# Token-major pieces of a gate stage: fixed order on vector and scalar engine, inverse roots as a one-column GpSimd power, early squares on the scalar engine

## The chip, the cores and the metric

The kernel runs on one core of one Trainium2 chip. A core has a matrix engine (TensorE, PE in the profile, with its weight loads as PEld), a vector engine (VectorE, DVE), a scalar engine for activation functions (ScalarE, ACT), a general engine (GpSimd, POOL), and SyncE (SP), whose queue issues nearly all transfers here. Each engine works through its own instructions in order and waits on semaphores for the others. The metric is the device time in microseconds (us), the median of several runs.

## The reference

One layer of a decoder block on x of 1024 tokens by 1024 features: a pooling mixer and a gated linear recurrence, an MLP with squared ReLU, a gated per-layer embedding, and a last RMS norm. What the change touches is the end:

```
z = rms_norm(h, norm_ple_g[l])
gate = jax.nn.sigmoid(z @ w_ple_gate[l] + b_ple_gate[l])
h = h + gate * (p[l] @ w_ple_proj[l])
...
return rms_norm(h, norm_final_g)
```

with `rms_norm(h, g) = h * rsqrt(mean(h * h) + 1e-6) * g`, the mean over the 1024 features of a token. All values are float32.

## The kernel before

Nearly everything is feature-major: `H[o]` holds feature block o (128 features on the partitions) for all 1024 tokens. Matrix products in float32 are made of three passes over operands split in a high and a low part (`split`, `mm`), which is why PE has the most work by far. A planner orders the instructions of each engine by their place in the program and by when their inputs are expected; what is wrapped in `keep_in_program_order` keeps the written order on its engine. The helper `pin` does that only while the list `in_order` is not empty.

The gate stage at the end runs in three parts.

1. First half of the tokens (group 0), feature-major, eight blocks: `ple_proj`, `ple_gate`, `ple_out`. The squares for the last norm are collected on the way.
2. Second half of the tokens (group 1), feature-major, but only the first four feature blocks, in the order 2, 3, 0, 1. In between, the first token half is scaled by its final norm (`finish`, called with the blocks that `DONE` lists) and stored (`store`, after blocks 3 and 7). The blocks of `H` for the second token half are turned token-major by `turn_block` (32 by 32 transposes), written to DRAM by `turn_out` and read back by `turn_in` as `late[i]`: 128 tokens on the partitions, 1024 features along the row. `quarter(i, 0)` is the row's early half (features that part 2 has finished), `quarter(i, 1)` its late half.
3. Second half of the tokens, late four feature blocks, token-major: four pieces i of 128 tokens. PE computes `token_proj` and `token_gate` of a piece into two PSUM banks. Then, per piece:
   - logits: gate product plus bias row (DVE, L1148), sigmoid (ACT, L1149), product with the projection (DVE, L1150), sum into the late half (`late_half`, DVE, L1143);
   - `early_half` for the early halves: a multiply-and-sum instruction on DVE gives the mean square plus epsilon (`mean`, L1109), then the early half is multiplied by its gains (L1117). It is called for pieces 0 and 1 in piece 0, for 2 in piece 1 and for 3 in piece 2;
   - `token_finish`: the mean square of the late half on top of the early one (`mean`), `root_of` (square root on ACT, L1155, then reciprocal on DVE, L1156), the early half scaled on ACT (L1163), the late half scaled by root and gains on DVE (L1164), and the store of the piece (L1165).

The last piece is `token_last`. Its gate product comes first, then its projection in two halves of 256 columns in banks of their own; the vector work follows in the same two halves, in written order, and the two halves of its output leave by separate stores (L1197). A one-column square root on `root` (L1175) makes ACT load the table of that function ahead of `root_of`.

PSUM banks are handed out in turn: pieces 0 and 2 use single banks, piece 1 a double one, and piece 3 three single banks. The means, roots and reciprocals are single columns of `spread`.

Of the kernel before, what the change touches and what calls it, by code (L numbers as in the profile page):

```python
# [31 lines left out]

ORDER = ((0, 1, 2, 3, 4, 5, 6, 7), (2, 3, 0, 1))

DONE = ((), (0, 1, 2), (3, 4), (5,), (6, 7), (), (), ())
FETCH = ((0, 1, 2, 3), (0, 1))
NTOK = 4
NQUAD = 4 * P
# [21 lines left out]
def block_kernel(  # L60
# [111 lines left out]
    def pin(ins):  # L172
        return tc.keep_in_program_order(ins) if in_order else ins
# [843 lines left out]
    rfin = T[5]  # L1017
    gate_p, held = {}, []
    ms = spread[:, 40 : 40 + 4 * NTOK]
    root = pool.tile([P, 1], F32, name="root")  # L1020

    def ple_psum(g, hs, o, apart):
        turn.append(o)
# [74 lines left out]
    def quarter(i, half):  # L1098
        return late[i][:, half * NQUAD : (half + 1) * NQUAD]
# [4 lines left out]
            quarter(i, half), bounce[half][i // 2][b : b + 4].rearrange("b t g x -> (b t) (g x)")  # L1104
        )

    def mean(i, x, before, to):

        nc.vector.tensor_tensor_reduce(  # L1109
            square[:, : x.shape[-1]] if len(x.shape) == 2 else square[:, :256].rearrange("p (g x) -> p g x", g=4),  # L1110
            x, x, 1.0 / D, before, ALU.mult, ALU.add, ms[:, to : to + 1],
        )

    def early_half(i):
        x = quarter(i, 0)
        mean(i, x, EPS, 4 * i)
        nc.vector.tensor_tensor(x, x, g_row[:, :NQUAD], ALU.mult)  # L1117

    def token_slice(i):
        return slice(HALF + i * P, HALF + (i + 1) * P)  # L1120
# [18 lines left out]
    def late_half(i, e, cut):  # L1139

        y = quarter(i, 1).rearrange("p (g o x) -> p g o x", g=4, x=32)[:, :, cut.start // P : cut.stop // P]
        e = e[:, cut].rearrange("p (o g x) -> p g o x", g=4, x=32)
        nc.vector.tensor_tensor(y, y, e, ALU.add)  # L1143

    def token_out_all(i, pg, pj):
        t, e = T[3 + i % 2][:, FIRST], T[3 + i % 2][:, SECOND]
        whole = slice(0, NQUAD)
        nc.vector.tensor_tensor(by(t, pg), got(pg), by(b_row, pg), ALU.add)  # L1148
        nc.scalar.activation(t, t, AF.Sigmoid)  # L1149
        nc.vector.tensor_tensor(by(e, pj), by(t, pj), got(pj), ALU.mult)  # L1150
        late_half(i, e, whole)

    def root_of(i):
        r = ms[:, 4 * i + 3 : 4 * i + 4]
        pin(nc.scalar.activation(r, ms[:, 4 * i + 2 : 4 * i + 3], AF.Sqrt))  # L1155
        pin(nc.vector.reciprocal(r, r))  # L1156
        return r

    def token_finish(i):
        mean(i, quarter(i, 1), ms[:, 4 * i : 4 * i + 1], 4 * i + 2)  # L1160
        r = root_of(i)
        x, y = quarter(i, 0), quarter(i, 1)
        nc.scalar.activation(x, x, AF.Identity, scale=r)  # L1163
        nc.vector.scalar_tensor_tensor(y, y, r, g_row[:, NQUAD:], ALU.mult, ALU.mult)  # L1164
        nc.sync.dma_start(token_out[:, i], late[i])  # L1165

    def token_last(i, pg, pj):

        t, e = T[3 + i % 2][:, FIRST], T[3 + i % 2][:, SECOND]
        cuts = slice(0, 256), slice(256, NQUAD)  # L1170
        in_order[:] = [True]
        for a, cut in enumerate(cuts):
            pin(nc.vector.tensor_tensor(t[:, cut], got(pg)[:, a], b_row[:, cut], ALU.add))
            pin(nc.scalar.activation(t[:, cut], t[:, cut], AF.Sigmoid))
        pin(nc.scalar.activation(root, t[:, -1:], AF.Sqrt))  # L1175
        at = 4 * i
        y = quarter(i, 1)
        for a, cut in enumerate(cuts):
            x = pj[a]
            pin(nc.vector.tensor_tensor(by(e[:, cut], x), by(t[:, cut], x), got(x), ALU.mult))  # L1180
            yv = y.rearrange("p (g o x) -> p g o x", g=4, x=32)[:, :, 2 * a : 2 * a + 2]
            ev = e[:, cut].rearrange("p (o g x) -> p g o x", g=4, x=32)
            pin(nc.vector.tensor_tensor(yv, yv, ev, ALU.add))
            pin(
                nc.vector.tensor_tensor_reduce(
                    square[:, :256].rearrange("p (g x) -> p g x", g=4),
                    *[y.rearrange("p (g x) -> p g x", g=4)[:, :, 64 * a : 64 * a + 64]] * 2,
                    1.0 / D, ms[:, at + a : at + a + 1], ALU.mult, ALU.add, ms[:, at + a + 1 : at + a + 2],
                )
            )  # L1190
        r = root_of(i)
        both = late[i].rearrange("p (h x) -> p h x", h=2)
        for cut in cuts:
            x, v = both[:, 0, cut], both[:, 1, cut]
            pin(nc.scalar.activation(x, x, AF.Identity, scale=r))
            pin(nc.vector.scalar_tensor_tensor(v, v, r, g_row[:, NQUAD:][:, cut], ALU.mult, ALU.mult))
            nc.sync.dma_start(token_out[:, i].rearrange("p (h x) -> p h x", h=2)[:, :, cut], both[:, :, cut])  # L1197
        in_order.clear()

    for g, hs in enumerate(GROUPS):  # L1200
        if g == 1:
            leave("ple")
            late[:] = space("late", 8, F32)
        for n, o in enumerate(ORDER[g]):
            pg, pj = ple_psum(g, hs, o, False)
            if g == 0 and n < 2:
                ple_gate(g, hs, o, pg, n == 1)
                held.append((o, pg, pj))
                if n == 0:
                    first_sums()  # L1210
                    continue
                for o, pg, pj in held:
                    ple_proj(hs, o, pj)
                for o, pg, pj in held:
                    ple_out(hs, o, pg, pj)
            else:
                ple_proj(hs, o, pj)
                ple_gate(g, hs, o, pg)
            if g == 0 and 1 <= n < 5:
                raw = wp.tile([P, S], F32, tag="raw", name=f"wg0_{n + 3}_raw")  # L1220
                nc.sync.dma_start(raw, w_gate[n + 3])
                x = slice((n - 1) * P, n * P)
                split(raw.rearrange("p (k x) -> p k x", k=NT), *(w[:, :, x] for w in quad))
            if g > 0 or n > 1:
                ple_out(hs, o, pg, pj, g == 0)
            if g == 0 and n > 0:
                for o in range(NT) if n == 1 else ():
                    norm2.add(H[o], SECOND)
                if n == 2:
                    norm2.rstd(R, norm2.sums((SECOND,)))  # L1230
                for o in LATER[n - 1]:
                    ple_in_normed(o, SECOND)
            if g == 1:
                for j in range(2):
# [12 lines left out]
                finish(DONE[n])  # L1247
                if n == 1:
                    nc.sync.dma_start(row[:, : S + NQUAD], rows.broadcast_to([P, S + NQUAD]))
    for i in range(NTOK):  # L1250
        end = i == NTOK - 1
        pg, pj = ple_psum(2, slice(0, NQUAD), i, end)
        if end:
            token_gate(i, pg)
            pj = [x[:, :256] for x in (pj, bank("ps_j_end"))]
            for a, x in enumerate(pj):
                token_proj(i, x, slice(256 * a, 256 * a + 256))
            token_last(i, pg, pj)
            continue
        token_proj(i, pj, slice(0, NQUAD))  # L1260
        token_gate(i, pg)
        token_out_all(i, pg, pj)
        for x in ((0, 1), (2,), (3,))[i]:
            early_half(x)
        token_finish(i)
        finish(DONE[4 + i])
    leave("late")
    leave("sums")
    leave("proj")
# [78 lines left out]
```

## Time and profile before

| | |
|---|---|
| median of 3 runs | 926.03 us (925.99 to 926.21) |
| profiled execution | 925.73 us, span 923.9 us |
| granted TensorE clock, mean | 0.996 |
| instructions in the span | 10987 |
| PE busy | 911.2 us (99%) |
| DVE busy | 763.7 us (83%) |
| ACT busy | 449.0 us (49%) |
| POOL busy | 5.6 us (1%), 7 instructions |

The span runs from the first to the last instruction of the profiled execution. A busy share is the engine's busy time over the span. In the rows of a timeline stand the start, the duration, the engine, the line of the program, the operation, what it writes and reads, the shape and how many instructions are merged into the row; in brackets, how long the engine had been idle before it and which instruction ended that idle time. "SPq" is SyncE's queue; its rows are the issue of transfers, not the transfers. In the table of groups the columns are busy time, mean duration in ns, and idle time before with its releaser.

### The profile page before, as it was taken

The numbers are of one execution on the slowest core, as the hardware profiler recorded it, in microseconds if no ns is written. First come the engines' busy times: TensorE is split into PE (matmuls) and PEld (weight loads), VectorE is DVE, ScalarE is ACT, GpSimd is POOL, SyncE is SP. The second block draws the span as 40 slices with busy tenths as digits, with TensorE's granted clock in tenths as the row PEclk, the third lists the DMA queues.
The fourth block names the chain that finished last, engine by engine and source line by source line (L and its number), as shares of the span: only waits on it lengthen the run. The fifth ranks groups of instructions, "written<-read, shape, count | busy, mean of one in ns | idle before, by whom it ended". The sixth has DMA issues, their size and how long they took to land.

```text
span 923.9 us, 10987 instructions
## 1 busy us (share of the span) xinstructions
PE 911.2 (99%) x4229; PEld 792.4 (86%) x4229; DVE 763.7 (83%) x921; ACT 449.0 (49%) x514; POOL 5.6 (1%) x7
## 2 busy tenths in 40 slices
PE   9999999999999999999999999999999999999994
PEld 7888888888888888888888888888888888888884
DVE  7997984669998888888888989979776579789656
ACT  7568892447543343334334554443444346555314
POOL 0000000002000000000000000000000000000000
PEclk9999999999999999999999999999999999999998
DMA  7211143112154355345434989366532441031452
GB/s 266 94 52 31 38 167 107 69 45 78 65 196 153 126 176 198 127 148 173 181 125 148 353 310 338 115 202 205 197 102 92 128 147 45 20 118 46 126 180 94
DMA packets 50036, 128.94 MB, mean 140 GB/s; under 512 B 4544, under 2 KB 10176, under 8 KB 49984
## 3 DMA queue, kind: packets, MB, share of 16 engines
q1 hardware_dynamic: 49840, 128.21, 40.7%
q8 instruction: 33, 0.54, 0.3%
q14 instruction: 19, 0.16, 0.1%
q10 hardware_dynamic: 144, 0.04, 0.0%
HBM read 92.58 MB, written 35.65 MB: 139 GB/s over the span
## 4 chain that ended last, share of the span: by engine, by line
PE 98%; DVE 1%; issue 0%; ACT 0%; ACTq 0%
PE ps_P_u L352 31%; PE ps_P_d L352 31%; PE ps_i L352 10%; PE ps_o L352 9%; PE ps_e L352 8%; PE ps_l L352 3%; PE ps_e L1126 2%; PE ps_j L352 1%; PE ps_g L566 1%; PE ps_p L352 1%; PE ps_l L482 0%; PE ps_j L1135 0%; DVE t L1109 0%; PE n_ps L418 0%; PE n_ps L419 0%
## 5 line engine op out<-in xcount | busy, mean ns | idle before, releaser
L352 PE MATMUL ps_P_d<-a,wd_P_hi 128*128 128x512 f32 x880 | 261.7, 379 | 0.0
L352 PEld LDWEIGHTS ps_P_d<-a,wd_P_hi 128*128 128x128 f32 x880 | 166.3, 189 | 23.6
L352 PE MATMUL ps_P_d<-a,wd_P_lo 128*128 128x512 f32 x440 | 166.8, 379 | 0.0
L352 PE MATMUL ps_P_u<-a,wu_hi 128*128 128x512 f32 x512 | 152.3, 379 | 0.0
L352 PE MATMUL ps_P_u<-y,wu_hi 128*128 128x512 f32 x384 | 114.2, 379 | 0.0
L352 PEld LDWEIGHTS ps_P_u<-a,wu_hi 128*128 128x128 f32 x512 | 96.8, 189 | 13.8
L352 PE MATMUL ps_P_u<-a,wu_lo 128*128 128x512 f32 x256 | 97.0, 379 | 0.0
L352 PEld LDWEIGHTS ps_P_d<-a,wd_P_lo 128*128 128x128 f32 x440 | 83.2, 189 | 11.8
L352 PEld LDWEIGHTS ps_P_u<-y,wu_hi 128*128 128x128 f32 x384 | 72.6, 189 | 10.3
L742 DVE TENSOR_TENSOR t<-t,ps_P_u 128x512 f32<-128x512 f32 (+1 forms) x80 | 62.6, 782 | 20.4 <-PE ps_P_u L352 20.4
L352 PE MATMUL ps_i<-a,wi_hi 128*128 128x512 f32 x288 | 74.3, 380 | 0.0
L352 PE MATMUL ps_P_u<-y,wu_lo 128*128 128x512 f32 x192 | 72.8, 379 | 0.0
L180 ACT ACTIVATE a<-wd 128x1024 fp32r<-128x1024 f32 x56 | 58.9, 1054 | 22.9 <-DMA wd<-act 14.5
L181 DVE TENSOR_TENSOR a<-wd,a 128x1024 fp32r<-128x1024 f32 x56 | 67.3, 1221 | 1.0 <-ACT a L180 0.6
L352 PE MATMUL ps_o<-y,wo_hi 128*128 128x512 f32 x256 | 65.7, 379 | 0.0
L352 PEld LDWEIGHTS ps_i<-a,wi_hi 128*128 128x128 f32 x288 | 54.1, 189 | 8.8 <-issue 1.0
L180 ACT ACTIVATE wu_hi<-wu 128x1024 fp32r<-128x1024 f32 x24 | 25.4, 1057 | 69.8 <-PE ps_P_u L352 44.2
L180 ACT ACTIVATE wu_hi<-wu_raw 128x1024 fp32r<-128x1024 f32 (+1 forms) x26 | 25.2, 974 | 66.3 <-PE ps_P_u L352 41.3
L352 PEld LDWEIGHTS ps_o<-y,wo_hi 128*128 128x128 f32 x256 | 48.4, 189 | 6.8
L352 PEld LDWEIGHTS ps_P_u<-a,wu_lo 128*128 128x128 f32 x256 | 48.4, 189 | 6.8
L180 ACT ACTIVATE wd_P_hi<-wd 128x1024 fp32r<-128x1024 f32 x24 | 25.3, 1054 | 48.6 <-PE ps_P_d L352 44.4
L742 DVE TENSOR_TENSOR h<-h,ps_P_d 128x512 f32<-128x512 f32 (+1 forms) x40 | 31.6, 790 | 19.1 <-PE ps_P_d L352 19.1
(251 smaller groups left out, 1480.8 us busy)
## 6 DMA issues: line engine op xcount, KB each, us to landing
wd<-act SPq DMA_DIRECT2D x56, 512.0 KB, 5.9
act<-t SPq DMA_DIRECT2D x32, 512.0 KB, 4.3
wu_raw<-in_w_up SPq DMA_DIRECT2D x16, 512.0 KB, 3.5
wu<-in_w_up SPq DMA_DIRECT2D x16, 512.0 KB, 4.0
act<-wu SPq DMA_DIRECT2D x16, 512.0 KB, 4.8
wd<-in_w_down SPq DMA_DIRECT2D x16, 512.0 KB, 6.5
h<-in_xT SPq DMA_DIRECT2D x14, 512.0 KB, 4.6
wg_raw<-in_w_gate SPq DMA_DIRECT2D x10, 512.0 KB, 3.3
```

Of the source, the lines that this page charges most:

```text
L180: first = pin(nc.scalar.activation(hi, src, AF.Copy))
L181: lowest[:] = [pin((eng or nc.vector).tensor_tensor(lo, src, f32(hi), ALU.subtract)).ins]
L352: ins = nc.tensor.matmul(ps, w, turns(z[:, hs]), start=first and z is zhi and w is whi, stop=last and w is wlo, skip_group_check=more,)
L566: nc.tensor.matmul(x, w[r, o * P : (o + 1) * P], turns(z[r, at : at + HALF]), start=n == 0, stop=n == 2)
L742: (eng or nc.vector).tensor_tensor(to, to if y is None else y, x, ALU.add)
L1126: nc.tensor.matmul(pg, z, turns(w[:, k]), start=k == n == 0, stop=k == NT - 1 and n == 2)
```

## The change

In the pieces of part 3:

- From piece 0 on, `in_order` is filled, so that the vector and scalar instructions of all four pieces keep the order in which they are written. GpSimd's instructions and the stores are not pinned.
- The square root on ACT and the reciprocal on DVE are replaced by one GpSimd instruction on one column, `means[i]` to the power -0.5 (`inverse`); a column `power` is set to -0.5 once by DVE. The column `root` and its square root are gone.
- The mean square of an early half is made by ACT: a square with scale D^-0.5 that sums along the row (`early_square`). DVE multiplies the early half by its gains as before and adds epsilon to the column (`early_gain`). This is done for pieces 0 and 1 in piece 0, and for 2 and 3 at the end of piece 1.
- The scaling of piece i and its store (`scale_late`, `scale_early`, `leave_for`) move to piece i + 1, behind that piece's logits and sigmoid; the late half of piece 2 is scaled at the end of piece 2.
- In the last piece the first half's square is made by ACT, with a one-column addition on DVE; the second half's stays on DVE.
- `finish` takes blocks 3, 4 and 5 in the third and 6 and 7 in the fourth block of part 2, where it took 3 and 4, 5, and (in piece 0) 6 and 7.

```diff
-DONE = ((), (0, 1, 2), (3, 4), (5,), (6, 7), (), (), ())
+DONE = (), (0, 1, 2), (3, 4, 5), (6, 7)
...
-    root = pool.tile([P, 1], F32, name="root")
+    early_mean, means, inverses = ([ms[:, 4 * x + i : 4 * x + i + 1] for i in range(NTOK)] for x in range(3))
+    power = pool.tile([P, 1], F32, name="power")
+    tc.keep_in_program_order(nc.vector.memset(power, -0.5))
...
+    def mean(i, cut=slice(0, NQUAD)):
+
+        n = cut.stop - cut.start
+        x = quarter(i, 1).rearrange("p (g x) -> p g x", g=4)[:, :, cut.start // 4 : cut.stop // 4]
+        pin(
+            nc.vector.tensor_tensor_reduce(
+                square[:, :n].rearrange("p (g x) -> p g x", g=4), x, x, 1.0 / D, early_mean[i], ALU.mult, ALU.add, means[i]
+            )
         )
 
-    def early_half(i):
+    def early_square(i):
+        pin(nc.scalar.activation(T[5][:, SECOND], quarter(i, 0), AF.Square, scale=D**-0.5, accum_out=early_mean[i]))
+
+    def early_gain(i):
         x = quarter(i, 0)
-        mean(i, x, EPS, 4 * i)
-        nc.vector.tensor_tensor(x, x, g_row[:, :NQUAD], ALU.mult)
+        pin(nc.vector.tensor_tensor(x, x, g_row[:, :NQUAD], ALU.mult))
+        pin(nc.vector.tensor_scalar_add(early_mean[i], early_mean[i], EPS))
...
+    def logits(i, pg, cut=slice(0, NQUAD)):
+        t = T[3 + i % 2][:, FIRST]
...
+        pin(nc.vector.tensor_tensor(by_a, got_a, bias, ALU.add))
+        pin(nc.scalar.activation(t[:, cut], t[:, cut], AF.Sigmoid))
+
+    def gated(i, pj, cut=slice(0, NQUAD)):
+
+        t, e = T[3 + i % 2][:, FIRST][:, cut], T[3 + i % 2][:, SECOND][:, cut]
+        pin(nc.vector.tensor_tensor(by(e, pj), by(t, pj), got(pj), ALU.mult))
+        y = quarter(i, 1).rearrange("p (g o x) -> p g o x", g=4, x=32)[:, :, cut.start // P : cut.stop // P]
+        pin(nc.vector.tensor_tensor(y, y, e.rearrange("p (o g x) -> p g o x", g=4, x=32), ALU.add))
+
+    def inverse(i):
+        nc.gpsimd.tensor_tensor(inverses[i], means[i], power, ALU.pow)
+
+    def scale_late(i, cut=slice(0, NQUAD)):
+        y = quarter(i, 1)[:, cut]
+        pin(nc.vector.scalar_tensor_tensor(y, y, inverses[i], g_row[:, NQUAD:][:, cut], ALU.mult, ALU.mult))
+
+    def scale_early(i, cut=slice(0, NQUAD)):
+        x = quarter(i, 0)[:, cut]
+        pin(nc.scalar.activation(x, x, AF.Identity, scale=inverses[i]))
+
+    def leave_for(i, cut=slice(0, NQUAD)):
+        to = token_out[:, i].rearrange("p (h x) -> p h x", h=2)
+        nc.sync.dma_start(to[:, :, cut], late[i].rearrange("p (h x) -> p h x", h=2)[:, :, cut])
 
     def token_last(i, pg, pj):
 
         cuts = slice(0, 256), slice(256, NQUAD)
...
+        for cut in cuts:
+            logits(i, pg, cut)
+        scale_early(i - 1)
+        leave_for(i - 1)
+        gated(i, pj[0], cuts[0])
+        y = quarter(i, 1).rearrange("p (g x) -> p g x", g=4)[:, :, :64]
+        pin(
+            nc.scalar.activation(
+                T[5][:, HALF : HALF + 256].rearrange("p (g x) -> p g x", g=4), y, AF.Square, scale=D**-0.5, accum_out=means[i - 1]
             )
+        )
+        gated(i, pj[1], cuts[1])
+        pin(nc.vector.tensor_tensor(early_mean[i], early_mean[i], means[i - 1], ALU.add))
+        mean(i, cuts[1])
+        inverse(i)
         for cut in cuts:
...
+            scale_early(i, cut)
+            scale_late(i, cut)
+            leave_for(i, cut)
...
+    in_order[:] = [True]
     for i in range(NTOK):
...
-        token_out_all(i, pg, pj)
-        for x in ((0, 1), (2,), (3,))[i]:
-            early_half(x)
-        token_finish(i)
-        finish(DONE[4 + i])
+        logits(i, pg)
+        if i > 0:
+            scale_late(i - 1)
+            scale_early(i - 1)
+            leave_for(i - 1)
+        gated(i, pj)
+        if i == 0:
+            for x in range(2):
+                early_square(x)
+                early_gain(x)
+        mean(i)
+        inverse(i)
+        if i == 1:
+            for x in range(2, NTOK):
+                early_square(x)
+                early_gain(x)
+        if i == 2:
+            scale_late(i)
+    in_order.clear()
```

More of the change, by code (lines that the diff above doesn't have):

```diff
@@ L1105, in turn_in @@
         )
[L1107 to L1111, printed above, removed]
-        )
-    def early_half(i):
+    def mean(i, cut=slice(0, NQUAD)):
[5 more added lines that the diff above has]
+            )
+        )
+    def early_square(i):
+        pin(nc.scalar.activation(T[5][:, SECOND], quarter(i, 0), AF.Square, scale=D**-0.5, accum_out=early_mean[i]))
+    def early_gain(i):
         x = quarter(i, 0)
-        mean(i, x, EPS, 4 * i)
-        nc.vector.tensor_tensor(x, x, g_row[:, :NQUAD], ALU.mult)
+        pin(nc.vector.tensor_tensor(x, x, g_row[:, :NQUAD], ALU.mult))
+        pin(nc.vector.tensor_scalar_add(early_mean[i], early_mean[i], EPS))
     def token_slice(i):
@@ L1143, in late_half @@
         nc.vector.tensor_tensor(y, y, e, ALU.add)
[L1145 to L1165, printed above, removed]
+    def logits(i, pg, cut=slice(0, NQUAD)):
+        t = T[3 + i % 2][:, FIRST]
+        got_a, by_a = (got(pg), by(t, pg)) if cut.stop - cut.start == NQUAD else (
+            got(pg)[:, cut.start // 256], t[:, cut]
+        )
+        bias = by(b_row, pg) if cut.stop - cut.start == NQUAD else b_row[:, cut]
+        pin(nc.vector.tensor_tensor(by_a, got_a, bias, ALU.add))
+        pin(nc.scalar.activation(t[:, cut], t[:, cut], AF.Sigmoid))
@@ L1167, in token_last @@
     def token_last(i, pg, pj):
-        t, e = T[3 + i % 2][:, FIRST], T[3 + i % 2][:, SECOND]
         cuts = slice(0, 256), slice(256, NQUAD)
[L1171 to L1189, printed above, removed]
-            )
@@ L1191, in token_last @@
-        r = root_of(i)
-        both = late[i].rearrange("p (h x) -> p h x", h=2)
-        for cut in cuts:
[L1194 to L1198, printed above, removed]
+        for cut in cuts:
+            logits(i, pg, cut)
@@ new lines, in token_last @@
+        scale_early(i - 1)
[5 more added lines that the diff above has]
+                T[5][:, HALF : HALF + 256].rearrange("p (g x) -> p g x", g=4), y, AF.Square, scale=D**-0.5, accum_out=means[i - 1]
+            )
+        )
+        gated(i, pj[1], cuts[1])
+        pin(nc.vector.tensor_tensor(early_mean[i], early_mean[i], means[i - 1], ALU.add))
+        mean(i, cuts[1])
```

## The prediction

> **What bounds the kernel now.** I read the page's busy shares first, then its chain of work that ended last, to learn whether any engine but TensorE (PE) can matter.
>
> ```profile
> PE 911.2 (99%) x4229; PEld 792.4 (86%) x4229; DVE 763.7 (83%) x921; ACT 449.0 (49%) x514; POOL 5.6 (1%) x7
> PE 98%; DVE 1%; issue 0%; ACT 0%; ACTq 0%
> ```
>
> PE is busy for nearly all of the span and carries 98% of the chain. The change touches no matmul, so only the few microseconds that PE does not carry can move. The busy time by windows around PE's end shows where they are.
>
> ```profile
> core 0: us, PE busy (x) PEld busy (x) DVE busy (x) ACT busy (x) POOL busy (x), PEclk, DMA share, GB/s
> 906.00:912.20 6.20, 6.20 (x35) 5.42 (x33) 6.20 (x16) 4.74 (x6) 0.00 (x0) 1.00 0.21 85
> 912.20:923.90 11.70, 0.01 (x1) 0.00 (x0) 5.85 (x17) 5.52 (x10) 0.00 (x0) 0.68 0.36 134
> ```
>
> Until 912.2 PE is full at full clock; VectorE (DVE) is full as well from 906. Behind PE lies a tail of 11.7 us. That tail is the question. The timeline of it (start, duration, engine, line):
>
> ```profile
> 900.34 10.52 PE L1126 MATMUL ps_e<-a 128*128 128x512 f32 x48
> ...
> 905.73 0.69 DVE L1148 TENSOR_TENSOR t<-ps_e,t 128x512 f32<-128x512 f32 x1 [1.30 <-PE ps_e L1126]
> ...
> 907.79 0.63 ACT L1149 ACTIVATE t<-t 128x512 f32<-128x512 f32 x1
> ...
> 908.94 0.68 DVE L1150 TENSOR_TENSOR t<-t,ps_j 128x512 f32<-128x512 f32 x1
> ...
> 910.15 0.69 DVE L1143 TENSOR_TENSOR late<-late,t 128x512 f32<-128x512 f32 x1
> ...
> 910.83 0.67 DVE L1117 TENSOR_TENSOR late<-late,t 128x512 f32<-128x512 f32 x1
> ...
> 911.37 0.83 PE L1135 MATMUL ps_j_end<-proj,proj 128*128 128x256 f32 x6
> ...
> 912.08 0.75 DVE L1109 CUSTOM_DVE_ANT_0 t<-late,edge 128x512 f32<-128x512 f32 x1
> 912.75 0.09 DVE L1109 DVE_READ_ACCUMULATOR2_ANT edge<- 128x1 f32 x1
> ...
> 913.30 0.75 DVE L1164 SCALAR_TENSOR_TENSOR late<-late,edge,t 128x512 f32<-128x512 f32 x1
> 913.97 0.75 DVE L1173 TENSOR_TENSOR t<-ps_e,t 128x256 f32<-128x256 f32 x2
> 914.47 1.28 ACT L1174 ACT_TABLE_LOAD   x1 [0.44 <-DVE t L1173]
> 915.76 0.72 ACT L1174 ACTIVATE t<-t 128x256 f32<-128x256 f32 x2
> 916.21 0.42 DVE L1180 TENSOR_TENSOR t<-t,ps_j 128x256 f32<-128x256 f32 x1 [1.49 <-ACT t L1174]
> ...
> 916.66 0.42 DVE L1183 TENSOR_TENSOR late<-late,t 128x256 f32<-128x256 f32 x1
> 917.12 0.48 DVE L1185 CUSTOM_DVE_ANT_1 t<-late,edge 128x256 f32<-128x256 f32 x1
> 917.53 0.08 DVE L1185 DVE_READ_ACCUMULATOR2_ANT edge<- 128x1 f32 x1
> ...
> 918.97 0.20 ACT L1155 ACTIVATE edge<-edge 128x1 f32<-128x1 f32 x1 [0.97 <-DVE edge L1185]
> 919.20 0.16 DVE L1156 RECIPROCAL edge<-edge 128x1 f32<-128x1 f32 x1 [0.27 <-ACT edge L1155]
> 919.40 0.88 DVE L1196 SCALAR_TENSOR_TENSOR late<-late,edge,t 128x256 f32<-128x256 f32 x2
> 919.40 0.91 ACT L1195 ACTIVATE late<-late,edge 128x256 f32<-128x256 f32 x2 [0.23 <-DVE edge L1156]
> 919.95 0.90 SPq L1197 DMA_DIRECT2D out<-late  x2
> ```
>
> The 48 matmuls that end at 910.86 are the gates of pieces 2 and 3. Piece 3's logits could start then; DVE gets to them at 913.97, 3.0 us late, because it still works off pieces 1 and 2. Next a table load of 1.28 us stands between logits and sigmoid, since ScalarE (ACT) had just taken a square root. Then a chain of 3.19 us runs from the first product (916.21) to the final scaling (919.40). From there to the end of the span are 4.5 us of scaling and stores; the change leaves these alone.
>
> **The change part by part.** Call p the time from the end of a mean to the start of the scaling that needs its inverse root, that is the one-column power on GpSimd (POOL) with both handovers, and L the start of piece 3's logits.
>
> *Table loads.* The roots were the only work that needed another table. Squares and sigmoids follow one another without a load:
>
> ```profile
> 863.23 0.63 ACT L391 ACTIVATE t<-h 128x512 f32<-128x512 f32 x1 [1.78 <-DVE h L1059]
> ...
> 867.16 0.67 ACT L1057 ACTIVATE t<-ps_e,vecs 128x512 f32<-128x512 f32 x1
> ```
>
> So the loads of the token stage go. One of them is on the path: 913.97 to 916.21 (2.24 us) becomes logits 0.43, sigmoid 0.42 and handovers of 0.03 to 0.04, that is 0.92. The preload of the root's table (L1175) was beside DVE work and is worth nothing.
>
> *DVE before L.* Piece 2's logits are ready at 905.73. In the new order: logits 0.69 to 906.42; sigmoid 0.63 to 907.09, with piece 1's late scaling on DVE under it; product 0.69 to 907.82; sum 0.69 to 908.54; mean 0.75 and its read to 909.40. Then the power, p, for which DVE waits, because piece 2's late scaling (one slot of 0.67 us, 913.30 to 913.97) stands in the order ahead of piece 3's logits. So L = max(910.9, 910.07 + p). What queues behind that wait is piece 3's logits, and behind them the whole end. ACT's sigmoid does not fill it.
>
> *Is DVE free at 905.73?* That depends on piece 1, and on the early halves, which come from DRAM:
>
> ```profile
> 893.06 0.82 SPq L1103 DMA_DIRECT2D late<-turn  x2
> ...
> 897.49 1.40 SPq L1103 DMA_DIRECT2D late<-turn  x2
> DMA to landing us min/median/max: 2.6/3.2/5.8
> 899.25 0.69 DVE L1148 TENSOR_TENSOR t<-ps_e,t 128x512 f32<-128x512 f32 x1 [3.67 <-PE ps_e L1126]
> L625 DVE TENSOR_TENSOR t<-t 128x1 f32<-128x1 f32 x1 | 0.2, 154 | 0.0
> L1163 ACT ACTIVATE late<-late,edge 128x512 f32<-128x512 f32 x3 | 2.2, 719 | 0.6 <-DVE edge L1156 0.6
> ```
>
> Halves 0 and 1 are asked for at 893.1 and 893.5 and land by the median 3.2 us later, at 896.7. Two squares of 0.63 on ACT, each gain 0.67 and each addition of epsilon 0.16 on DVE, then piece 0's mean: DVE is through at 899.5, so piece 1's logits slip 0.25 us from 899.25. The sigmoid ends at 900.9. Late scaling 0 needs the first power (899.55 + p); then product and sum 1.38, mean 0.84, and for halves 2 and 3 (landed by 901.5, squared on ACT behind early scaling 0, by 903.1) two gains and additions, 1.66. With p = 0.8 DVE is done at 904.9. That leaves 0.8 us of slack, so p up to 1.6 costs nothing here. A read of ACT's accumulator has no row; between 0 and the 0.20 of ACT's one-column row it stays hidden in the early squares.
>
> *The end.* From L: first half's logits and sigmoid 0.92; product and sum 0.42 each with a handover, to L + 1.79; second product 0.33 behind the first sum (two logits of 0.42 took 0.75), to L + 2.12; sum to L + 2.57; column addition 0.16 to L + 2.76; one half-wide mean 0.41 (917.12 to its read) and read 0.08 to L + 3.31, roundings and handovers included. ACT does early scaling 2 (0.72) up to L + 1.9 and the first half's square up to L + 2.4, with an accumulator read L + 2.6: just in time. If that read costs 0.2 more, the end is 0.2 later. Then p, then the scaling.
>
> *p itself.* No power and no one-column arithmetic of POOL is in the trace. The nearest rows are POOL's own:
>
> ```profile
> 0.24 0.10 POOL L1334 MEMSET const-float32-0.0<- 128x1 f32 x1 [0.24 <-issue]
> 211.58 1.98 POOL L217 TENSOR_TENSOR rstd<-wu_raw 128x512 f32<-128x512 f32 x1 [211.14 <-DMA wu_raw<-in_w_up]
> 213.64 2.14 POOL L217 TENSOR_TENSOR rstd<-rstd,wu_raw 128x512 f32<-128x512 f32 x1
> 215.74 1.28 POOL L217 TENSOR_TENSOR wu_raw<-wu_raw,wu_raw 128x512 f32<-128x512 f32 x1
> ```
>
> Below: 0.10, a one-column write. Above: 2.14, a full-width sum. One column is nearer to the first in size, but a power is more arithmetic than a sum; I take the middle of 0.10 and 1.28 (the row without a busy DVE beside it), 0.7, plus two handovers of 0.05: p = 0.8. Where the power is slower than the root and reciprocal it replaces (918.97 to 919.40), the part is a loss.
>
> *Stores and the first half's finish.* Both stores of the first half are on the queue long before the pieces end, though the program asks for the last two blocks of it only in piece 0; asking in the fourth block instead moves nothing that PE waits for:
>
> ```profile
> 880.69 3.63 SPq L1067 DMA_DIRECT2D out<-h  x2
> ```
>
> On SP the store of a piece now comes one piece later in the text, behind the transposed loads, which are all issued by 898.9; piece 2's store leaves about 3 us before the last two. Cost nothing; if the last stores had to share with it, at most its overlap.
>
> *Sum.* With p = 0.8: L = 910.93, scaling at 910.93 + 3.31 + 0.80 = 915.04 instead of 919.40, a gain of 4.36: 3.04 by the earlier logits, 1.32 by the load, and 3.31 + 0.80 - 0.92 = 3.19 is what the last chain took before, so it breaks even. The profiled execution took 925.73 with a span of 923.9; 925.73 - 4.36 = 921.4. The median of the runs is 0.30 above the profiled one, so 921.7.
>
> *A rule against it.* POOL's first sum in the trace took 1.98, its third 1.28, so at most 0.7 us could be a first call's price, and that fits into the slack above. The Trainium skill, GPSIMD Engine Reference, section Instruction dispatch, says that the first call to a freshly loaded GpSimd kernel pays a code load of about 6 us, invisible in the profile. By the row the sum stays 921.7; by that page's figure, as an estimate, 4.36 - (6 - 0.8) makes it 0.8 us slower than before. No row here shows such a load for a plain tensor operation.
>
> **The rivals.** A difference under 0.2% (1.85 us) is about what a measurement of this kernel can't tell from none.
>
> *Power as dear as a full tile.* p = 2.14. Piece 2's logits slip by 0.54, L = 912.75, scaling 918.2, gain 1.2: 924.5 by the profile, 924.8 by the median. For it: power is software work on an engine whose rows are slow. Against: one column is 1/512 of those rows.
>
> *First power late, once.* Of a delay x, 0.8 is slack, the rest delays piece 2 and so the end: gain 4.36 - (x - 0.8), level at x = 5.2. Time near 926.0 there. Against it: the first POOL row above. What the Trainium skill's GPSIMD Engine Reference says under Instruction dispatch would make x large.
>
> *Slower: DVE, held in fixed order by every power.* If p is above 2.5, late scaling 0 holds piece 1's product, late scaling 1 holds piece 2's, and p counts at each. For p = 4: power 0 ends 903.55, piece 1's mean 906.5, piece 2's logits start 908.2, power 1 ends 910.5, piece 2's mean 913.4, power 2 at 917.4, L = 918.1, scaling 925.4: 6.0 us slower, 932.0. Level at p = 2.5, over 0.2% slower from about 3. For it: no row bounds a power; against: both POOL ends above are below it.
>
> *The order waits for data.* If halves 0 and 1 took the 5.8 us maximum, mean 0 ends at 901.7, piece 1 slips 2.2, of which 0.8 is slack: gain 3.0, 923.1. The median speaks against it.
>
> **How the numbers follow.** Forecast 0.70, from p = 0.1 (gain 5.06, 921.0) to p = 1.6 (L = 911.67, gain 2.82, 923.2). Dear power 0.10, first power late 0.06, slower 0.10, late data 0.04. Faster: 0.70 + 0.04 = 0.74; same: 0.16; slower: 0.10. The range from 920.9 to 924.8 takes in both ends of p and leaves out the late first power and the slower case, 0.16.
>
> **What would show it.** Right: no table load on ACT in the pieces; piece 3's logits within 0.3 us of 910.9; four one-column POOL rows under 1 us; the final scaling near 915.0; PE's last matmul still at 912.2. Wrong: a POOL row of 2 us or more, DVE idle ahead of a late scaling with POOL as releaser, a long first power, or DVE still busy with piece 2 at 912.

## The result and the profile after

The changed kernel takes 921.82 us (median of 6 runs, 921.07 to 921.97) where the kernel before takes 926.19 us (median of 6, 925.99 to 926.87) beside it: a ratio of 0.995, 95% interval 0.9937 to 0.9963, or 4.37 us. The forecast was 921.7.

The profiled execution took 921.81 us with a span of 920.0 us. First the two lines of its page that answer to those of before:

```profile
PE 911.1 (99%) x4229; PEld 793.0 (86%) x4229; DVE 762.5 (83%) x913; ACT 444.3 (48%) x514; POOL 8.4 (1%) x11
PE 98%; DMA 1%; issue 1%; DVE 0%; ACT 0%; SPq 0%; POOLq 0%; POOL 0%; ACTq 0%
```

PE has the same work; POOL has four instructions more. ACT's busy time is 4.7 us lower: the five table loads of the pieces (1.28 us each) and the roots are gone, and the squares have come. DVE's busy time is only 1.2 us lower, so on DVE the gain is not less work but another place for it. The timeline of the end (start, duration, engine, line):

```profile
898.18 0.95 SPq L1105 DMA_DIRECT2D late<-turn  x2
...
899.58 0.55 POOL L1170 TENSOR_TENSOR edge<-edge,power 128x1 f32<-128x1 f32 x1 [681.99 <-DVE edge L1114]
...
900.56 0.74 DVE L1174 SCALAR_TENSOR_TENSOR late<-late,edge,t 128x512 f32<-128x512 f32 x1
...
901.05 10.52 PE L1134 MATMUL ps_e<-a 128*128 128x512 f32 x48
...
903.63 0.94 POOL L1170 TENSOR_TENSOR edge<-edge,power 128x1 f32<-128x1 f32 x1 [3.50 <-DVE edge L1114]
...
904.74 0.14 DVE L1125 TENSOR_SCALAR edge<-edge 128x1 f32<-128x1 f32 x1
906.43 0.69 DVE L1159 TENSOR_TENSOR t<-ps_e,t 128x512 f32<-128x512 f32 x1 [1.54 <-PE ps_e L1134]
...
909.95 0.08 DVE L1114 DVE_READ_ACCUMULATOR2_ANT edge<- 128x1 f32 x1
910.11 0.55 POOL L1170 TENSOR_TENSOR edge<-edge,power 128x1 f32<-128x1 f32 x1 [5.54 <-DVE edge L1114]
910.70 0.75 DVE L1174 SCALAR_TENSOR_TENSOR late<-late,edge,t 128x512 f32<-128x512 f32 x1 [0.66 <-POOL edge L1170]
...
911.61 0.76 DVE L1159 TENSOR_TENSOR t<-ps_e,t 128x256 f32<-128x256 f32 x2 [0.16 <-PE ps_e L1134]
912.07 0.75 ACT L1160 ACTIVATE t<-t 128x256 f32<-128x256 f32 x2 [3.67 <-DVE t L1159]
912.08 0.83 PE L1143 MATMUL ps_j_end<-proj,proj 128*128 128x256 f32 x6
912.52 0.42 DVE L1165 TENSOR_TENSOR t<-t,ps_j 128x256 f32<-128x256 f32 x1
...
914.71 0.08 DVE L1114 DVE_READ_ACCUMULATOR2_ANT edge<- 128x1 f32 x1
914.87 0.55 POOL L1170 TENSOR_TENSOR edge<-edge,power 128x1 f32<-128x1 f32 x1 [4.21 <-DVE edge L1114]
915.45 0.91 ACT L1178 ACTIVATE late<-late,edge 128x256 f32<-128x256 f32 x2 [1.46 <-POOL edge L1170]
```

The bracket of the row at 911.61 is the main reading: piece 3's logits wait 0.16 us for PE, not PE's result for DVE as before. Behind them stands the sigmoid with no table load, and the last scaling starts at 915.45 instead of 919.40.

PE itself came 0.71 us later in this execution (last matmul to 912.91, before 912.20): it waited for its first operands, 0.42 us for ACT at 7.62 us and 0.30 us for DVE at 8.41 us, and did not in the execution of before. In the profiles below, one execution each, the end of the last matmul lies between 912.2 and 913.5, and not always for this reason: in finish_late PE waits 0.7 us for DVE (`wd_P_lo`) in the middle of the kernel. These waits lie far ahead of the stage that the change touches, so I compare the tail, from the end of the last matmul to the end of the span: 11.70 us before, 7.09 after, 4.61 less.

### The profile page after: what moved, and what is told of

Its sections match the earlier page's. It is cut to its first block, busy times and chain, and to the rows that moved or that the text cites. A ratio compares the mean times of both kernels' runs of the same rounds, so it can differ in the third digit from the quotient of the medians.

```text
span 920.0 us, 10987 instructions
## 1 busy us (share of the span) xinstructions
PE 911.1 (99%) x4229; PEld 793.0 (86%) x4229; DVE 762.5 (83%) x913; ACT 444.3 (48%) x514; POOL 8.4 (1%) x11
## 4 chain that ended last, share of the span: by engine, by line
PE 98%; DMA 1%; issue 1%; DVE 0%; ACT 0%; SPq 0%; POOLq 0%; POOL 0%; ACTq 0%
PE ps_P_d L352 32%; PE ps_P_u L352 32%; PE ps_i L352 10%; PE ps_o L352 9%; PE ps_e L352 8%; PE ps_l L352 3%; PE ps_e L1134 2%; PE ps_j L352 1%; PE ps_g L566 1%; PE ps_p L352 1%; DMA h<-in_xT 1%; PE ps_j L1143 0%; PE n_ps L419 0%; PE n_ps L418 0%; PE ps_e L1143 0%
```

## The experiments

The theory: the gain is DVE's time. The new text lets DVE take piece 3's logits when PE delivers them; everything else is small or hidden. The first rival: the gain is the power, through the table loads that it makes unnecessary. The second: it is the relief of DVE by squares on ACT. A third question came up on the way: what the small move of `finish` does.

| kernel | median, us | ratio to before, 95% interval | last matmul ends | span | tail |
|---|---|---|---|---|---|
| before | 926.19 | | 912.20 | 923.9 | 11.70 |
| changed | 921.82 | 0.995 (0.9937 to 0.9963) | 912.91 | 920.0 | 7.09 |
| power_alone | 925.26 | 0.9991 (0.9982 to 0.9999) | 912.22 | 923.2 | 10.98 |
| root_in_order | 921.90 | 0.9952 (0.9938 to 0.9965) | 913.00 | 920.4 | 7.40 |
| order_alone | 924.83 | 0.9985 (0.9976 to 0.9994) | 912.19 | 922.6 | 10.41 |
| dve_squares | 921.70 | 0.9953 (0.9941 to 0.9966) | 913.48 | 920.6 | 7.12 |
| free_load | 922.64 | 0.9963 (0.9951 to 0.9975) | 912.74 | 921.0 | 8.26 |
| unpinned | 922.61 | 0.9961 (0.9948 to 0.9975) | 912.67 | 920.8 | 8.13 |
| power_six | 930.62 | 1.0049 (1.0037 to 1.0062) | 912.20 | 928.4 | 16.20 |
| first_power_late | 925.12 | 0.9990 (0.9981 to 0.9998) | 912.42 | 923.4 | 10.98 |
| finish_late | 925.63 | 0.9996 (0.9987 to 1.0005) | 913.20 | 924.4 | 11.20 |
| finish_late_loads_first | 922.24 | 0.9960 (0.9947 to 0.9974) | 913.25 | 921.1 | 7.85 |
| finish_late_pinned | 921.39 | 0.9950 (0.9937 to 0.9962) | 912.57 | 919.7 | 7.13 |

The kernel before was measured beside each group of them, with medians of 925.96 to 926.19. The last three columns are from one profiled execution each.

### The power alone

```diff
 # kernel before
     def root_of(i):
         r = ms[:, 4 * i + 3 : 4 * i + 4]
-        pin(nc.scalar.activation(r, ms[:, 4 * i + 2 : 4 * i + 3], AF.Sqrt))
-        pin(nc.vector.reciprocal(r, r))
+        nc.gpsimd.tensor_tensor(r, ms[:, 4 * i + 2 : 4 * i + 3], power, ALU.pow)
         return r
...
-        pin(nc.scalar.activation(root, t[:, -1:], AF.Sqrt))
```

> The kernel before with one part of the change: the square root and reciprocal become the one-column power on GpSimd, and the preload of the root's table goes. Order theory (most of the gain is that VectorE comes to piece 3's logits 3 us earlier, and that needs the new order): the planner still puts both early halves and two late scalings between the logits of pieces 2 and 3, some 8.0 us of VectorE work instead of 8.24, so the logits move only 0.3 us; the table load of 1.3 us leaves the path; the last chain is 0.2 us longer. Gain 1.4 us, 924.8. Rival (the power and the table loads are the gain): 3 us or more of the 4.4, 923.2 or less.

Measured: 925.26, 0.76 us faster than the median of before beside it (926.02), about half of what was expected and far from the rival's 3 us. The timeline between the logits of piece 3 and what holds them:

```profile
909.26 0.94 POOL L1156 TENSOR_TENSOR edge<-edge,power 128x1 f32<-128x1 f32 x1 [4.18 <-DVE edge L1110]
...
910.23 0.75 DVE L1164 SCALAR_TENSOR_TENSOR late<-late,edge,t 128x512 f32<-128x512 f32 x1 [0.45 <-POOL edge L1156]
...
913.65 0.75 DVE L1164 SCALAR_TENSOR_TENSOR late<-late,edge,t 128x512 f32<-128x512 f32 x1 [0.66 <-POOL edge L1156]
914.32 0.75 DVE L1173 TENSOR_TENSOR t<-ps_e,t 128x256 f32<-128x256 f32 x2
...
915.28 0.42 DVE L1179 TENSOR_TENSOR t<-t,ps_j 128x256 f32<-128x256 f32 x1 [0.21 <-ACT t L1174]
```

The loads are gone: from piece 3's logits to the first product it is 0.96 us (914.32 to 915.28) where it was 2.24. But the logits come at 914.32, later than the 913.97 of before, and the chain behind them is 0.2 us longer. In the planner's order a late scaling stands right behind its mean, and DVE waits there for POOL, 0.45 us at 910.23 and 0.66 us at 913.65. I had counted DVE's work between the logits of pieces 2 and 3, and not these waits. The power is a gain for ACT that the old order partly gives back on DVE.

### Root and reciprocal again, in the new order

```diff
 # changed kernel
-        nc.gpsimd.tensor_tensor(inverses[i], means[i], power, ALU.pow)
+        pin(nc.scalar.activation(inverses[i], means[i], AF.Sqrt))
+        pin(nc.vector.reciprocal(inverses[i], inverses[i]))
```

> The changed kernel with square root on ScalarE and reciprocal on VectorE again, in the fixed order; everything else as changed. The table loads come back, two for each of the four pieces save one. Order theory: the loads run while VectorE does products, sums and means, so piece 3's logits stay at PE's end; only the last root waits, for its load behind the first half's square, 0.3 us: 922.1. Rival (power and loads are the gain): a load returns to the path, 1.3 us for one and 2.6 for two: 923.1 to 924.4.

Measured: 921.90, within 0.1 us of the changed kernel; its tail is 0.31 us longer, as the theory said. So in this order the power is worth 0.1 us by the median, 0.3 by the tail. The timeline shows how cheap the loads are here:

```profile
910.16 0.20 ACT L1170 ACTIVATE edge<-edge 128x1 f32<-128x1 f32 x1 [0.36 <-DVE edge L1114]
910.38 1.28 ACT L1160 ACT_TABLE_LOAD   x1
...
911.70 0.76 DVE L1159 TENSOR_TENSOR t<-ps_e,t 128x256 f32<-128x256 f32 x2 [0.36 <-PE ps_e L1134]
912.16 0.75 ACT L1160 ACTIVATE t<-t 128x256 f32<-128x256 f32 x2 [0.50 <-DVE t L1159]
```

The load of the sigmoid's table starts at 910.38, right behind the root, and is over at 911.66, before the logits that the sigmoid needs are there.

### The order with all old operations

```diff
 # changed kernel, with the edit of root_in_order, and
     def early_square(i):
-        pin(nc.scalar.activation(T[5][:, SECOND], quarter(i, 0), AF.Square, scale=D**-0.5, accum_out=early_mean[i]))
+        x = quarter(i, 0)
+        pin(nc.vector.tensor_tensor_reduce(square, x, x, 1.0 / D, EPS, ALU.mult, ALU.add, early_mean[i]))
...
-        pin(nc.vector.tensor_scalar_add(early_mean[i], early_mean[i], EPS))
 # and in token_last the first half's square by tensor_tensor_reduce on DVE
```

> The changed kernel with all old operations in the new order: root and reciprocal, early squares on VectorE, and the last piece's first half squared on VectorE. Order theory: piece 2's logits slip by 0.8 us as VectorE has more to do, piece 3's by 0.4, the last chain is 0.2 longer: 922.5, so that 3.7 of the 4.4 us stay. Rival (power and loads, or the relief of VectorE by ScalarE, are the gain): 924 or more.

Measured: 924.83, a gain of 1.2 us instead of 3.5. The theory as it stood fell here: the order alone does not carry the gain, although root_in_order shows that the power can go, and the next run that ACT's early squares can. The timeline shows a new wait:

```profile
906.56 0.68 DVE L1159 TENSOR_TENSOR t<-ps_e,t 128x512 f32<-128x512 f32 x1
...
907.33 1.28 ACT L1160 ACT_TABLE_LOAD   x1 [3.60 <-DVE t L1159]
908.62 0.63 ACT L1160 ACTIVATE t<-t 128x512 f32<-128x512 f32 x1
...
912.63 0.75 DVE L1159 TENSOR_TENSOR t<-ps_e,t 128x256 f32<-128x256 f32 x2
913.12 1.28 ACT L1160 ACT_TABLE_LOAD   x1 [1.40 <-DVE t L1159]
914.42 0.72 ACT L1160 ACTIVATE t<-t 128x256 f32<-128x256 f32 x2
```

Here the table load has a releaser, DVE's logits: ACT was idle for 3.60 and 1.40 us ahead of it and still didn't load. In the compiled program the sigmoid of pieces 2 and 3 has two waits, one for the logits and one for ACT's own earlier writing of the same tile, and the one for the logits stands at the load in front of it (DVE_49 and Activation_49 are the counters that DVE and ACT raise as they finish work):

```
order_alone    L1160 ACT_TABLE_LOAD [waits DVE_49]
order_alone    L1160 ACTIVATE t<-t 128x512 [waits Activation_49]
root_in_order  L1160 ACT_TABLE_LOAD
root_in_order  L1160 ACTIVATE t<-t 128x512 [waits DVE_49]
```

In root_in_order ACT's squares come in between; one of them has waited for ACT itself already, so the sigmoid has one wait left, and the load none. So far this is an argument from the listing; the run free_load tests it.

### The early squares on DVE

```diff
 # changed kernel, with only the edit of early_square and early_gain shown above
```

> The changed kernel with the four early mean squares on VectorE again, epsilon inside them; power and order as changed. Order theory: VectorE is idle for 1.5 us before piece 2's logits, and the squares of two halves, less the additions of epsilon, take 1.2 there: within 0.15 us of the changed kernel, 921.8 to 922.0. Rival (the relief of VectorE is the gain): 2.4 us of VectorE work return, 923 to 924.

Measured: 921.70, no difference (tail 7.12 against 7.09). DVE had room: in the changed kernel it is idle for 1.5 us ahead of piece 2's logits (the rows at 904.74 and 906.43). As a relief of DVE, ACT's early squares are worth nothing here.

### Freeing the table load

```diff
 # order_alone
         pin(nc.vector.reciprocal(inverses[i], inverses[i]))
+        for _ in range(2 if i < NTOK - 1 else 0):
+            pin(nc.scalar.activation(T[5][:, S - 1 :], power, AF.Copy))
```

> order_alone with two one-column copies on ScalarE behind the root in the first three pieces. In order_alone the sigmoid of pieces 2 and 3 waits both for the logits and for ScalarE's own earlier writing of the same tile, and the table load ahead of it starts only when the logits are done (907.33 and 913.12). The second copy waits for the first and so takes that second wait over; the load is then free to run early. Theory of the waiting load: both loads leave the path, piece 3's logits go from 912.63 to 911.3 and 1.3 us more are saved behind them: 2.66 us faster than order_alone, 922.2. Rival (order_alone lost its gain to VectorE's extra work and to the roots themselves): unchanged, 924.8, or slower by the copies.

Measured: 922.64, 2.19 us faster than order_alone by two useless copies per piece. The rows that answer to those of order_alone:

```profile
904.83 1.28 ACT L1160 ACT_TABLE_LOAD   x1
...
908.04 0.63 ACT L1160 ACTIVATE t<-t 128x512 f32<-128x512 f32 x1 [1.92 <-DVE t L1159]
...
911.50 1.28 ACT L1160 ACT_TABLE_LOAD   x1
...
912.05 0.75 DVE L1159 TENSOR_TENSOR t<-ps_e,t 128x256 f32<-128x256 f32 x2
912.79 0.72 ACT L1160 ACTIVATE t<-t 128x256 f32<-128x256 f32 x2
```

The loads start at 904.83 and 911.50, without a releaser. So the wait at the load, and not the load or the root, was most of what order_alone lost: 2.2 of 3.0 us. The new theory: the gain needs both DVE's early logits and a sigmoid with no table load waiting in front of it; for the second the power is enough, and so are other ACT instructions in between. Of the 0.4 us that are missing to the 922.2 expected, 0.3 are at 912.79: the second load ends that much after the first half of piece 3's logits.

### Without the pins

```diff
 # changed kernel
-    in_order[:] = [True]
     for i in range(NTOK):
...
 # token_last sets it for itself
```

> The changed kernel without the fixed order in pieces 0 to 2 (the last piece keeps it, as before the change); the program text, the power and ScalarE's squares stay. The planner puts both early gains of pieces 2 and 3 between the logits of piece 2 and their sum, 1.4 us of VectorE work, of which 0.66 fits under the sigmoid. Theory (operations and their place in the text make the gain, the pins little): piece 3's logits slip 0.5 us, 922.3. Rival (the pins are the gain): 924 or more.

Measured: 922.61, 0.8 us slower than the changed kernel; expected were 0.5. Most of the loss is not where it was expected:

```profile
900.81 10.52 PE L1134 MATMUL ps_e<-a 128*128 128x512 f32 x48
...
906.34 0.75 DVE L1174 SCALAR_TENSOR_TENSOR late<-late,edge,t 128x512 f32<-128x512 f32 x1 [0.45 <-POOL edge L1170]
...
907.01 0.68 DVE L1159 TENSOR_TENSOR t<-ps_e,t 128x512 f32<-128x512 f32 x1
...
912.48 0.75 DVE L1159 TENSOR_TENSOR t<-ps_e,t 128x256 f32<-128x256 f32 x2
```

Counted from the start of PE's last gates, piece 2's logits come after 6.20 us (5.38 in the changed kernel) and piece 3's after 11.67 (10.56). So 0.8 of the 1.1 us are lost ahead of piece 2, where DVE still works off pieces 0 and 1 and waits 0.45 us for POOL; the early gains behind piece 2's logits cost the other 0.3. Most of the gain holds with the planner's own order; the pins add the last 0.8 us. This run keeps the new text, the power, ACT's squares and the earlier finish together, so it does not show which of them the planner needs.

### A dear power, and a late first one

```diff
 # changed kernel, power_six; first_power_late has ten, for i == 0 alone
         nc.gpsimd.tensor_tensor(inverses[i], means[i], power, ALU.pow)
+        for _ in range(5):
+            nc.gpsimd.tensor_tensor(inverses[i], inverses[i], ones_f[:, :1], ALU.pow)
```

> The changed kernel with every power followed by five more powers of exponent 1 on the same column, so that p, the time from mean to scaling, is 3.7 us instead of 0.66. The slower rival of the prediction (fixed order holds VectorE at every power): 903.2, 909.8, 916.4 and 924.0 for the four inverses, scaling 8.6 us later than in the changed kernel: 930.4. If the order hid the powers of the first three pieces, only the last one would count: 3.0 us more, 924.8.

> The changed kernel with ten more powers of exponent 1 behind the first piece's power alone, as a first call that is 6.2 us late. By the prediction's working with the changed kernel's own slack (VectorE was idle for 1.54 us before piece 2's logits): piece 1's product waits, piece 2's logits come at 910.6 and piece 3's at 915.55, 3.9 us later: 925.8, so about the time before. If one late power were hidden by the three pieces behind it: 921.8.

Measured: 930.62 and 925.12. Both are slower than the changed kernel by nearly what the working says, 8.8 us (8.6 expected) and 3.3 us (3.9). DVE's waits for POOL in them:

```profile
902.47 0.75 DVE L1176 SCALAR_TENSOR_TENSOR late<-late,edge,t 128x512 f32<-128x512 f32 x1 [2.53 <-POOL edge L1172]
...
909.55 0.75 DVE L1176 SCALAR_TENSOR_TENSOR late<-late,edge,t 128x512 f32<-128x512 f32 x1 [2.29 <-POOL edge L1172]
...
916.22 0.75 DVE L1176 SCALAR_TENSOR_TENSOR late<-late,edge,t 128x512 f32<-128x512 f32 x1 [3.79 <-POOL edge L1172]
```

```profile
899.73 6.19 POOL L1172 TENSOR_TENSOR edge<-edge,ones 128x1 f32<-128x1 f32 x10
...
905.96 0.75 DVE L1176 SCALAR_TENSOR_TENSOR late<-late,edge,t 128x512 f32<-128x512 f32 x1 [5.80 <-POOL edge L1172]
```

The slower rival of the prediction was a real mechanism with nearly the right price: in the fixed order DVE stops at every late scaling whose power is not done. What decides is the power's size, and for pieces 2 and 3 it is 0.55 us.

### The finish of the first half at its old place

```diff
 # changed kernel
-DONE = (), (0, 1, 2), (3, 4, 5), (6, 7)
+DONE = ((), (0, 1, 2), (3, 4), (5,), (6, 7), (), (), ())
...
         if i == 2:
             scale_late(i)
+        finish(DONE[4 + i])
```

> The changed kernel with the first half's finish asked for at its old places: blocks 3 and 4 in the third, 5 in the fourth block, 6 and 7 after piece 0. The prediction costs this part at nothing, since the planner runs all eight scalings by 884 either way: 921.8, within 0.2 us of the changed kernel. Rival (the earlier finish keeps a store and two scalings of VectorE out of the pieces): 1.4 us of VectorE work return to piece 0, piece 1 slips by 1 us, of which 0.5 is left at piece 2: 922.3 or more.

Measured: 925.63; 3.8 of the 4.4 us are gone. That is against the theory, and the rival's working had only 0.5 us; nor is the rival's cause there, as the eight scalings run before 885 on DVE in this kernel too. The difference is elsewhere. The timeline around pieces 0 and 1:

```profile
900.25 0.69 DVE L1159 TENSOR_TENSOR t<-ps_e,t 128x512 f32<-128x512 f32 x1 [3.67 <-PE ps_e L1134]
900.86 0.68 DVE L1124 TENSOR_TENSOR late<-late,t 128x512 f32<-128x512 f32 x1
...
901.34 10.52 PE L1134 MATMUL ps_e<-a 128*128 128x512 f32 x48
...
904.44 0.36 SPq L1182 DMA_DIRECT2D out<-late  x1
...
905.27 0.84 SPq L1105 DMA_DIRECT2D late<-turn  x2
...
908.94 0.63 ACT L1120 ACTIVATE t<-late 128x512 f32<-128x512 f32 x1 [4.62 <-DMA late<-turn]
...
911.12 0.68 DVE L1159 TENSOR_TENSOR t<-ps_e,t 128x512 f32<-128x512 f32 x1
```

Two orders changed. Piece 1's logits (900.25) stand ahead of piece 0's early gain (900.86), although both are pinned in the other order. And on SP's queue the store of piece 0 (904.44), which waits for its scaling, stands ahead of the last two transposed loads (905.27; in the changed kernel 898.18). ACT waits 4.62 us for that data, and piece 2's logits come at 911.12. Counted from PE's last gates (901.34 here, 901.05 in the changed kernel) that is 4.4 us later. Two runs take the two apart:

```diff
 # finish_late_loads_first: finish_late, with both stores held in program order on SP
-        nc.sync.dma_start(first_out[:, os], h_all[:, os, FIRST])
+        pin(nc.sync.dma_start(first_out[:, os], h_all[:, os, FIRST]))
 # and the same around the store in leave_for
 # finish_late_pinned: finish_late, with finish's scalings pinned
-            nc.vector.scalar_tensor_tensor(hv, hv, col("g_fin", o), rfin[:, FIRST], ALU.mult, ALU.mult)
+            pin(nc.vector.scalar_tensor_tensor(hv, hv, col("g_fin", o), rfin[:, FIRST], ALU.mult, ALU.mult))
```

> finish_late with the stores of the first half and of the pieces held in program order on the queue, so that the last two transposed loads are issued ahead of piece 0's store again; on VectorE the logits of piece 1 still stand ahead of the early gains of piece 0, as in finish_late. Theory (two things cost finish_late 3.8 us: the store, which waits for its scaling, holds the loads behind it on the queue from 898 to 905; and piece 1's logits, hoisted over the early gains, put piece 0's mean 3.3 us later): loads at 898, piece 2's logits 1.4 us later than in the changed kernel, 923.1. Rival (the hoisted logits alone are the loss, the loads wait in their shadow): unchanged, 925.6. Second rival (the queue alone): 921.8.

> finish_late with the scalings of blocks 6 and 7 pinned too, so that the written order in the pieces has no gap: piece 1's logits stand behind piece 0's mean again, and VectorE does 1.4 us of scaling ahead of them. Theory (finish_late is slow because an instruction that is not pinned breaks the fixed order, not because of the work): piece 1's logits slip 0.95 us, and 1.5 us of idle time ahead of piece 2's take that up: 921.9. Rival (VectorE's 1.4 us or the 1 MB store in the pieces are what costs): 923 or more.

Measured: 922.24 and 921.39. The first has its last two loads at 898 again:

```profile
898.22 1.39 SPq L1105 DMA_DIRECT2D late<-turn  x2
```

With that, 3.4 us come back: the queue was most of the loss (2.5 expected), the hoisted logits the other 0.4 (0.8 by the tail). With the scalings pinned, all of it comes back, though DVE now does 1.4 us of scaling in the middle of piece 0:

```profile
899.05 1.41 DVE L1077 SCALAR_TENSOR_TENSOR h<-h,vecs,t 128x512 f32<-128x512 f32 x2
899.21 0.99 POOL L1170 TENSOR_TENSOR edge<-edge,power 128x1 f32<-128x1 f32 x1 [681.97 <-DVE edge L1114]
...
900.37 0.68 DVE L1159 TENSOR_TENSOR t<-ps_e,t 128x512 f32<-128x512 f32 x1
```

So neither the work nor the store costs anything here: DVE is still idle for 0.79 us ahead of piece 2's logits. The pair shows that an instruction that isn't pinned, standing between two pinned ones in the text, opens a gap over which the next one can be hoisted; that the pin holds an instruction only behind its direct predecessor in the text explains this, and it fits both orders, but I know it only from them. Why the planner then put piece 0's store ahead of the loads is open. finish_late_pinned has the changed kernel's tail (7.13 against 7.09); in its profile PE ends 0.34 us earlier (912.57 against 912.91), so I don't call it the faster kernel for its lower median.

## Why the prediction was right, and where it was wrong

- *What bounds, and where the change can act.* Right. PE's work is unchanged, and the tail shrank by 4.61 us where 4.36 were forecast. PE's later start took 0.71 of that back in the profiled execution. By that shift the signs that the prediction gave as times are missed on the clock (logits at 911.61 and not within 0.3 of 910.9, PE's end at 912.91); counted from PE's gates they hold.
- *L, the start of piece 3's logits.* Right: PE's gate plus 0.04 us, no backlog. DVE reached the end of piece 2's mean at 910.03, 3.60 us after piece 2's logits began; the working had 3.67.
- *The end.* From L to the last power's mean 3.18 us (working 3.31), p = 0.66 (working 0.80). From PE's gate to the scaling 3.88 us, working 4.18. ACT's accumulator reads took 0.19 us each, at the upper end given, and stayed hidden. That 921.7 and 921.82 agree to 0.1 us is partly luck: these terms were up to 0.14 us too large each, and no term had PE's 0.71 us.
- *p.* The middle between a one-column write and a full-width sum was close by luck as much as by reason: no row of before bounded a power. The prediction's working lost the whole gain at 2.5 us; no run stands there, but power_six, with 3.8 us from mean to scaling, is 4.5 us slower than the kernel before.
- *Is DVE free at piece 2?* Right, with 1.5 us of slack instead of 0.8: piece 1's logits were expected to slip 0.25 us and instead waited 0.45 us for PE. That is one reason why a first power that was 6.2 us late cost 3.3 us (3.9 by the tail) and not the 5.4 that 0.8 us of slack would give.
- *Table loads, 1.32 us of the sum.* The number was right and the credit only half: from L to the first product it is 0.91 us now, 2.24 before. The step said that the roots' loads go because the roots go. But root_in_order keeps the roots and loses 0.1 us (0.3 by the tail), so it is not the load that costs but a load whose start is tied to the logits. And the power alone does not keep the 1.32 us: power_alone took the load off the path and gave 0.55 back, 0.35 by later logits and 0.2 in the last chain.
- *Stores and finish, "cost nothing".* This step failed, though the time came out right. It looked at where the scalings run, found them early in either case, and never asked what their place in the text does to the order of what is pinned around them and of SP's queue. Undone, it costs 3.8 us. The forecast of DVE's order held only because the change has this part in it; the prediction did not know that it needed it, and that is luck.
- *Code load at the first call.* No run shows one. The first power took 0.55 us, as did the third and fourth, and the late scaling that needs it began at 900.56, 1.06 us after the mean, without a wait. A first power that was 6.2 us late cost 3.3 us (first_power_late). The prediction's row against such a load was misread: it allowed 0.7 us for a first call, from POOL's first and third sum (1.98 and 1.28 us), but in the changed kernel the first took 1.28 us and the third 2.26. The Trainium skill, GPSIMD Engine Reference, section Instruction dispatch, has about 6 us for the first call of a freshly loaded kernel; no run here shows such a load for this operation.

## What to carry to other kernels

In a tail, read every row's releaser, table loads too: a load with a releaser cannot use the idle time that stands before it, and an unrelated small instruction of the same engine can free it. Whether it is on the path is told by who waits behind it: in the kernel before, DVE's product at 916.21 waited 1.49 us behind the load at 914.47, but DVE never waited behind the one at 906.49, which had a releaser too. When an order is written out by hand, an instruction left to the planner in the middle of it counts as part of the order, on the queue of the transfers as well. A slow engine may take a one-column step if what it delays is taken up by idle time on the waiting engine: work that out by the waiting engine's order, not by the step's own time.

## What the runs showed of the hardware

- A one-column power on GpSimd took 0.55 us with DVE idle, and 0.93 to 1.06 us in nine cases in which it started beside a running DVE instruction, eight of them with two tiles from SBUF as inputs: in the changed kernel the second one (903.63) runs beside the early gain and takes 0.94, and in finish_late the same power, with DVE idle, takes 0.55. In all nine the power ended 0.40 to 0.42 us after the end of the DVE instruction beside which it had started, as if most of it had to wait for that end. The number of inputs does not explain every case: beside a mean square, which names one full tile, a power took 1.06 us in dve_squares (904.21) and 0.55 in unpinned (904.49).

```profile
906.55 0.55 POOL L1170 TENSOR_TENSOR edge<-edge,power 128x1 f32<-128x1 f32 x1 [2.99 <-DVE edge L1114]
```

The Trainium skill, GPSIMD Engine Reference, section Key points, says that GpSimd shares its SBUF interfaces with VectorE and names two SBUF inputs as a case of contention. The runs agree for the DVE instructions that name two tiles; for the mean square they are divided. The powers on the path, those of pieces 2 and 3, ran beside an idle DVE.
- Chained powers of one column took 0.62 us each (6.19 us for ten).
- A table load of 1.28 us delayed the next sigmoid by its full length or by 0.3 us at most, by the wait that it carries (order_alone and free_load, which differ by two one-column copies in each of the first three pieces; the 0.3 us are piece 3's).
